# Attention scores of a head pair: two 64-row products on the halves of the array instead of one 128-row product over zero-padded keys

## The chip, the cores and the metric

The kernel runs on one core of a Trainium2 chip. The metric is device time in microseconds (us): 629.18 us, the median of 3 runs (628.95, 629.18, 633.04).

## What is computed

Two layers (DEPTH = 2) of an encoder on 256 tokens of width 1024. Each layer is an attention sublayer with 16 heads of 64 dimensions in three groups, followed by a gated feed-forward sublayer. All inputs and outputs are 32-bit floats. The attention part of the reference, cut to what matters here:

```python
qa = rms_norm(heads(qa, 4), qg[0]);  ka = rms_norm(heads(ka, 4), kg[0])
out_a = neighbourhood_attention(qa, ka, heads(va, 4), ...)   # group "a": 4 heads, bias and mask
qd, kd = partial_rotary(rms_norm(...)), partial_rotary(rms_norm(...))
out_d = dilated_window_attention(qd, kd, heads(vd, 6), ...)  # group "d": 6 heads, mask
qc, kc = axial_rotary(rms_norm(...)), axial_rotary(rms_norm(...))
out_c = gqa_block_attention(qc, kc, heads(vc, 2))            # group "c": 6 query heads on 2 key heads
...
s = einsum('bqhd,bqkhd->bhqk', q, k) * scale + bias          # the scores of one head: 256 x 256, over 64 dimensions
p = softmax(s);  o = p @ v
x = x + concat(rms_norm(out_a), rms_norm(out_d), rms_norm(out_c)) @ w_out
...
x = x + (gelu(conv(rms_norm(x) @ w_g)) * (rms_norm(x) @ w_u)) @ w_dn
```

## The kernel before

Every matrix product is made in three parts to keep the accuracy of 32-bit floats: each operand is split into a high part, rounded to the format that TensorE takes in one pass (fp32r), and the rest, a low part; `mm3` (line 544) multiplies high by high, high by low and low by high into the same PSUM tile. ScalarE writes each high part (a cast), VectorE the low part (a subtraction). This holds for the weights (`split`, line 516) as for the activations.

**Order of the work.** The program first writes all operations down (`Plan.add`, line 233) and then plans the order itself (`Plan.order`, line 278): it simulates the five engines with the costs of `cost` (line 348) and hand-over times between engines, and always takes next the operation that could begin earliest, ties going to the one written first. The result is a fixed order for each engine; an engine that comes to an operation whose inputs are missing waits there, and everything behind it waits too. PSUM tiles come from two pools of four banks: `psa` for long accumulations, `psw` for everything short, the scores among it.

**Attention of a layer.** Queries and keys of a group are normed and rotated with tokens on the partitions, then transposed on TensorE in 128-column pieces, each of which holds a pair of heads (64 + 64 rows), so a pair's 64 + 64 dimensions lie on the 128 partitions. `transposed` (line 856) moves them out of PSUM: ScalarE the high part, VectorE the low part. For the queries (`queries`, line 868) one copy takes all 128 rows. For the keys (`keys`, line 876) there are two, of 64 rows each: the tiles `kown` and `kkv` (lines 469 and 470; `const_ko` and `const_kc` in the profile) hold for each pair two blocks of 256 columns, one with the first head's keys on the upper 64 rows and zeros below, one with the second head's keys on the lower 64 rows and zeros above. The zeros are written once at the start by GpSimd (lines 471 to 473).

`scores` (line 1053) makes the scores of a pair of heads: for each of the two blocks of 128 query tokens, t, the 128-row queries of both heads are the stationary operand and the 512 columns of keys beside zeros the moving one; so one `mm3` gives the scores of both heads side by side in one PSUM tile. That is 6 products of 128 rows and 512 columns for a pair, 48 for a layer, 96 in all. A PSUM tile holds block t of both heads.

`Head.softens` (line 906) is the softmax on VectorE and ScalarE: maximum over each block t (with the bias added for groups "d" and "a"), `small_nm` from both maxima, exponentials, division. `Head.turn` (line 937) transposes the probabilities on TensorE into a `psw` tile and splits them into `act_ch` and `act_cl`; `Head.weigh` (line 953) multiplies them with the values (products of 256 columns). The loop at line 1123 writes, for each head i: the scores of a pair, the turn of head i-1, the weighing of head i-2. Behind it, as filler on TensorE, stand the products of the remaining projections (`psa_a<-...,act_hT`) and of the output projection (`psa_a<-...,act_mixT`), which the planner puts wherever TensorE would be free.

The feed-forward sublayer and the first projections of a layer use none of this.

## Time and profile before

| | |
|---|---|
| median of 3 runs | 629.18 us (628.95 to 633.04) |
| the profiled execution | 629.88 us |
| its span, first to last instruction | 627.9 us |
| TensorE clock granted | 1.0 throughout |
| TensorE products of the scores | 60 of `const_ko`, 36 of `const_kc`; the first starts at 42.7, the last at 418.0 us |
| attention of layer 0, of layer 1 | about 42 to 127 us, 345 to 432 us |

PE is TensorE's matmul stream, PEld its stream of weight loads (every matmul has one), DVE is VectorE, ACT is ScalarE, POOL is GpSimd. The ends of matmuls in the trace are modelled: matmuls follow each other faster than they "last", so how long one takes of the engine is read from the distance between two starts. A row of the timeline gives the start, the time from it to the end of the last instruction of the row, and the number of instructions merged into it. Shapes stand as rows*columns of the stationary operand, then what is written.

### The profile page before, as it was taken

What the parts mean: (1) busy time and instruction counts of PE and PEld (TensorE: products, weight loads), DVE (VectorE), ACT (ScalarE), POOL (GpSimd) and SP (SyncE); (2) the same over time, 40 slices, a digit from 0 to 9 for tenths busy, and PEclk for the clock granted to TensorE, in tenths of its full rate; (3) what the DMA queues carried; (4) which work ended last, traced back from release to release, by engine and by line L of the source; (5) the groups of instructions that cost most, each with busy time, mean ns of one, the idle gap of its engine ahead of it and who ended that gap; (6) DMA issues with size and microseconds to landing.
All of it is one profiled execution on the core that took longest, in us unless ns stands there. A gap on an engine that the chain in (4) does not pass through costs nothing.

```text
span 627.9 us, 9711 instructions
## 1 busy us (share of the span) xinstructions
PE 613.9 (98%) x3400; PEld 531.4 (85%) x3400; DVE 497.6 (79%) x1038; ACT 436.5 (70%) x1076; POOL 90.8 (14%) x139
## 2 busy tenths in 40 slices
PE   8998999989999999999999999999999999999997
PEld 6997898878888888888899989787888888888886
DVE  4899989889777777777877898988887777777775
ACT  6887998786665556656678989887766655666552
POOL 5765231340000000000013210311000000000000
PEclk9999999999999999999999999999999999999999
DMA  8794311694556655555435732134655555555511
GB/s 283 253 282 143 114 36 41 214 237 164 194 200 202 200 183 176 182 197 185 149 109 165 248 102 85 35 117 155 202 200 201 195 175 171 198 200 181 171 51 67
DMA packets 81344, 104.65 MB, mean 167 GB/s; under 512 B 9464, under 2 KB 68952, under 8 KB 81296
## 3 DMA queue, kind: packets, MB, share of 16 engines
q1 hardware_dynamic: 80720, 103.51, 51.0%
q8 instruction: 26, 0.43, 0.3%
q10 hardware_dynamic: 576, 0.53, 0.3%
q14 instruction: 22, 0.18, 0.1%
HBM read 102.54 MB, written 1.49 MB: 166 GB/s over the span
## 4 chain that ended last, share of the span: by engine, by line
PE 88%; DVE 7%; ACT 2%; issue 1%; DMA 1%; POOL 0%; ACTq 0%; DVEq 0%
PE psw_w L345 47%; PE psa_a L345 41%; DVE wp_lo L345 2%; DVE act_s2k L345 1%; DMA const_x<-in_x_dram 1%; DVE act_z L345 1%; DVE act_hT L345 1%; ACT act_s2k L345 1%; DVE small_mx L345 0%; DVE small_ss L345 0%; DVE small_nm L345 0%; DVE act_cl L345 0%; DVE const_ko L345 0%; DVE const_x L345 0%; ACT wp_hi L345 0%
## 5 line engine op out<-in xcount | busy, mean ns | idle before, releaser
L345 DVE TENSOR_TENSOR wp_lo<-wp_raw,wp_hi 128x512 fp32r<-128x512 f32 (+2 forms) x348 | 247.4, 740 | 48.8 <-ACT wp_hi L345 47.0
L345 PE MATMUL psw_w<-act_hT,wp_hi 128*128 128x512 f32 x704 | 247.3, 396 | 4.3 <-DVE act_hT L345 4.3
L345 ACT CAST wp_hi<-wp_raw 128x512 fp32r<-128x512 f32 (+2 forms) x348 | 212.9, 659 | 22.8 <-PE psw_w L345 15.5
L345 PE MATMUL psw_w<-act_hT,wp_lo 128*128 128x256 f32 x704 | 195.9, 279 | 0.0
L345 PEld LDWEIGHTS psw_w<-act_hT,wp_hi 128*128 128x128 f32 x704 | 131.8, 188 | 36.1 <-DVE act_hT L345 5.5
L345 PEld LDWEIGHTS psw_w<-act_hT,wp_lo 128*128 128x128 f32 x704 | 132.6, 188 | 1.2
L345 PE MATMUL psa_a<-wp_hi,act_hT 128*128 128x384 f32 (+2 forms) x448 | 114.8, 334 | 0.0
L345 ACT COPY act_s2k<-psw_w 128x256 f32<-128x256 f32 x88 | 32.4, 373 | 80.3 <-PE psw_w L345 80.3
L345 PEld LDWEIGHTS psa_a<-wp_hi,act_hT 128*128 128x128 f32 x448 | 79.3, 191 | 2.4
L345 PE MATMUL psa_a<-wp_lo,act_hT 128*128 128x384 f32 (+2 forms) x224 | 75.1, 335 | 0.0
L345 PE MATMUL psa_a<-wp_lo,act_ch 128*128 128x512 f32 x176 | 69.5, 395 | 0.0
L345 PE MATMUL psa_a<-wp_hi,act_ch 128*128 128x512 f32 x176 | 69.5, 395 | 0.0
L345 PE MATMUL psa_a<-wp_hi,act_cl 128*128 128x512 f32 x176 | 66.2, 395 | 0.3 <-DVE act_cl L345 0.3
L345 DVE TENSOR_TENSOR act_s2k<-psw_w,act_s2k 128x256 f32<-128x256 f32 x88 | 36.8, 422 | 30.7 <-ACT act_s2k L345 30.2
L345 PEld LDWEIGHTS psa_a<-wp_lo,act_hT 128*128 128x128 f32 x224 | 42.6, 190 | 2.6 <-DVE wp_lo L345 1.4
L345 PEld LDWEIGHTS psa_a<-wp_hi,act_cl 128*128 128x128 f32 x176 | 33.1, 188 | 8.5 <-DVE act_cl L345 0.8
L345 PEld LDWEIGHTS psa_a<-wp_hi,act_ch 128*128 128x128 f32 x176 | 33.1, 188 | 7.9 <-ACT act_ch L345 0.2
L345 PEld LDWEIGHTS psa_a<-wp_lo,act_ch 128*128 128x128 f32 x176 | 33.1, 188 | 6.9
L345 DVE SCALAR_TENSOR_TENSOR act_s2k<-act_s2k,act_cw,act_s2k 128x255 f32<-128x255 f32 x88 | 36.7, 477 | 1.4 <-ACT act_s2k L345 1.3
L345 ACT ACTIVATE act_s2k<-act_s2k,act_cw 128x256 f32<-128x256 f32 x44 | 24.1, 595 | 13.6 <-DVE act_s2k L345 13.6
L345 POOL TENSOR_TENSOR small_rstd<-small_ms,const_mh 128x6 f32<-128x6 f32 (+2 forms) x26 | 31.3, 1204 | 2.1
L345 ACT ACTIVATE act_s2k<-act_s2k 128x512 f32<-128x512 f32 x22 | 13.9, 633 | 22.5 <-DVE act_s2k L345 22.5
(112 smaller groups left out, 818.5 us busy)
## 6 DMA issues: line engine op xcount, KB each, us to landing
wp_raw<-in_w_gate_up_dram SPq DMA_DIRECT2D x44, 1024.0 KB, 5.0
wp_raw<-in_w_down_dram SPq DMA_DIRECT2D x22, 1024.0 KB, 4.7
wp_raw<-in_w_in_dram SPq DMA_DIRECT2D x14, 768.0 KB, 4.8
wp_raw<-in_w_in_dram SPq DMA_DIRECT2D x8, 1024.0 KB, 5.9
wp_raw<-in_w_out_dram SPq DMA_DIRECT2D x8, 768.0 KB, 4.6
wp_raw<-in_w_out_dram SPq DMA_DIRECT2D x4, 512.0 KB, 3.7
act_nab<-dram_scr SPq DMA_DIRECT2D x4, 448.0 KB, 8.0
out_dram<-const_x SPq DMA_DIRECT2D x4, 256.0 KB, 2.0
```

The lines of the kernel that those rows point to most:

```text
L345: getattr(o.engine.real, o.method)(*map(real, o.args), **{k: real(v) for k, v in o.kw.items()})
```

## The change

- Keys lose the zeros: one tile of 128 rows for a pair, as the queries have (`act_ko`, `act_kc` in place of `const_ko`, `const_kc`), filled by one copy on ScalarE and one subtraction on VectorE per block of tokens, both over 128 rows. `queries` and `keys` become one function, `by_pairs`. The memsets of the zeros go.
- Scores: a product takes one head's 64 rows, which are the upper (LOW) or lower (HIGH) half of the array's rows, and 256 columns of keys. For a pair there are 2 heads x 2 blocks t x 3 parts = 12 products in place of 6, alternating between the halves. A PSUM tile holds both blocks of one head.
- Burst: the planner gets `together`. The 12 products of a pair stand behind each other on TensorE with nothing between, and the first is placed only when the inputs of all 12 and both PSUM tiles are there. The planner's cost of a product with fewer than 128 rows is n / 4.8 + 15 ns.

Where this moves instructions. TensorE at the first pair of heads of layer 0 (`psw_w` are the score tiles, `act_qo` the queries; `psa_a` is filler); before, the first two products of the pair and, after twenty-two of filler, the other four:

```order
L345 MATMUL psa_a_344<-wp_hi_247,act_hT_138 128x384
L345 MATMUL psw_w_125<-const_ko_117,act_qo_452 128x512
L345 MATMUL psw_w_125<-const_ko_145,act_qo_452 128x512
L345 MATMUL psa_a_314<-wp_lo_258,act_hT_138 128x384
...
L345 MATMUL psa_a_344<-wp_hi_247,act_hT_138 128x384
L345 MATMUL psw_w_125<-const_ko_117,act_qo_459 128x512
L345 MATMUL psw_w_149<-const_ko_117,act_qo_452 128x512
L345 MATMUL psw_w_149<-const_ko_145,act_qo_452 128x512
L345 MATMUL psw_w_149<-const_ko_117,act_qo_459 128x512
L345 MATMUL psa_a_160<-wp_hi_133,act_hT_138 128x256
```

and now:

```order
L393 MATMUL psa_a_332<-wp_hi_235,act_hT_135 128x384
L393 MATMUL psw_w_123<-act_ko_574,act_qo_440 128x256
L393 MATMUL psw_w_144<-act_ko_574,act_qo_440 128x256
L393 MATMUL psw_w_123<-act_ko_584,act_qo_440 128x256
L393 MATMUL psw_w_144<-act_ko_584,act_qo_440 128x256
L393 MATMUL psw_w_123<-act_ko_574,act_qo_447 128x256
L393 MATMUL psw_w_144<-act_ko_574,act_qo_447 128x256
...
L393 MATMUL psw_w_144<-act_ko_584,act_qo_440 128x256
L393 MATMUL psw_w_123<-act_ko_574,act_qo_447 128x256
L393 MATMUL psw_w_144<-act_ko_574,act_qo_447 128x256
L393 MATMUL psa_a_154<-wp_hi_130,act_hT_135 128x256
```

The twelve products stand in one piece, where the last four stood before; their two PSUM tiles take turns.

VectorE at the same place, from the keys' low parts (`const_ko`, `act_ko`) to the maxima of the first head (`small_mx`, `small_nm`); the ISA rows add the bias and take the maximum. Before:

```order
L345 TENSOR_TENSOR const_ko_145<-psw_w_149,const_ko_117 64x3x128 x2
L345 TENSOR_TENSOR const_ko_145<-psw_w_121,const_ko_117 64x3x128 x2
L345 TENSOR_TENSOR wp_lo_258<-wp_raw_170,wp_hi_247 128x384 x4
L345 TENSOR_TENSOR wp_lo_143<-wp_raw_93,wp_hi_133 128x512 x4
L345 ISA act_s2k_202,small_mx_671<-psw_w_125,const_dil_219 128x256
L345 ISA small_mx_671 128x1
L345 TENSOR_TENSOR wp_lo_258<-wp_raw_141,wp_hi_247 128x512
L345 ISA act_s2k_202,small_mx_671<-psw_w_149,const_dil_219 128x256
L345 ISA small_mx_671 128x1
L345 TENSOR_SCALAR small_nm_692<-small_mx_671 128x2
```

and now:

```order
L393 TENSOR_TENSOR act_ko_584<-psw_w_144,act_ko_574 128x3x128
L393 TENSOR_TENSOR act_ko_584<-psw_w_119,act_ko_574 128x3x128
L393 TENSOR_TENSOR wp_lo_246<-wp_raw_164,wp_hi_235 128x384 x4
L393 TENSOR_TENSOR wp_lo_140<-wp_raw_93,wp_hi_130 128x512 x4
L393 TENSOR_TENSOR wp_lo_246<-wp_raw_138,wp_hi_235 128x512
L393 ISA act_s2k_190,small_mx_673<-psw_w_123,const_dil_207 128x256
L393 ISA small_mx_673 128x1
L393 ISA act_s2k_190,small_mx_673<-psw_w_123,const_dil_207 128x256
L393 ISA small_mx_673 128x1
L393 TENSOR_SCALAR small_nm_690<-small_mx_673 128x2
```

Four subtractions for the keys became two, and one split of weights (`wp_lo`) that stood between the two maxima now stands ahead of both; both maxima read the one tile of the first head.

TensorE at the first pair of group "c" in layer 0 (`const_ident,act_s2k` are the transposes of a head's probabilities). Before, the products of the pair stood among the transposes of the head before:

```order
L345 MATMUL psw_w_149<-const_ident_81,act_s2k_123 128x128
L345 MATMUL psw_w_89<-const_kc_173,act_qc_782 128x512
L345 MATMUL psw_w_149<-const_ident_81,act_s2k_123 128x128 x3
L345 MATMUL psw_w_89<-const_kc_190,act_qc_782 128x512
L345 MATMUL psw_w_89<-const_kc_173,act_qc_791 128x512
L345 MATMUL psw_w_121<-const_kc_173,act_qc_782 128x512
```

and now they stand ahead of them:

```order
L393 MATMUL psa_a_154<-wp_lo_246,act_hT_135 128x256
L393 MATMUL psw_w_123<-act_kc_1016,act_qc_762 128x256
L393 MATMUL psw_w_119<-act_kc_1016,act_qc_762 128x256
...
L393 MATMUL psw_w_123<-act_kc_1016,act_qc_784 128x256
L393 MATMUL psw_w_119<-act_kc_1016,act_qc_784 128x256
L393 MATMUL psw_w_89<-const_ident_81,act_s2k_150 128x128 x4
```

The transposes of that head, four in a row, now come after the whole burst.

The diff, cut to its core:

```diff
@@ class Plan
+    @contextmanager
+    def together(self):
+
+        self.burst = len(self.bursts)
+        self.bursts[self.burst] = []
+        yield
+        self.burst = None
...
@@ Plan.order
+        def at_of_burst(burst):
+            at, wanted = 0.0, {}
+            members = set(self.bursts[burst])
+            for i in self.bursts[burst]:
+                o = ops[i]
+                if any(j not in members and not gone[j] for j in o.before):
+                    return None
+                at = max(at, o.at, free[o.engine.name])
+                for t in o.tiles:
+                    if t.slot is not None:
+                        at = max(at, t.since)
+                    else:
+                        wanted.setdefault(t.pool, set()).add(t)
+            for s, tiles in wanted.items():
+                if {t.turn for t in tiles} != set(range(s.given, s.given + len(tiles))) or len(s.free) < len(tiles):
+                    return None
+                at = max(at, sorted(s.free)[len(tiles) - 1][0])
+            return at
...
                     o = ops[i]
+                    if e in opened:
+                        if o.burst != opened[e]:
                             continue
+                        at = at_of(o)
+                    elif o.burst is not None:
+                        at = at_of_burst(o.burst) if i == self.bursts[o.burst][0] else None
+                    else:
+                        at = at_of(o)
...
+            if o.burst is not None:
+                opened[e] = o.burst
+                if i == self.bursts[o.burst][-1]:
+                    del opened[e]
...
@@ cost
+        if args[1].shape[0] < P:
+            return n / 4.8 + 15, 0
         return n / (2.4 if args[1].dtype == F32R else 1.2) + 2.5, 0
...
-    LOW, HIGH = slice(0, HD), slice(HD, P)
-    kown = [const.tile([P, H_DIL // 2, 2, S], F32R, tag=f"ko{i}", name=f"ko{i}") for i in range(2)]
-    kkv = [const.tile([P, H_GKV, 2, S], F32R, tag=f"kc{i}", name=f"kc{i}") for i in range(2)]
-    for z in kown + kkv:
-        nc.gpsimd.memset(z[HIGH, :, 0].bitcast(F32), 0.0)
-        nc.gpsimd.memset(z[LOW, :, 1].bitcast(F32), 0.0)
...
-            for rows_, *both in places:
-                h, o = (z[:, :, t * P : (t + 1) * P] for z in both)
-                nc.scalar.copy(h, pv[rows_])
-                nc.vector.tensor_tensor(o, pv[rows_], h.bitcast(F32), op=ALU.subtract)
...
+            h, o = (z[:, :, t * P : (t + 1) * P] for z in both)
+            nc.scalar.copy(h, pv)
+            nc.vector.tensor_tensor(o, pv, h.bitcast(F32), op=ALU.subtract)
+
+        def by_pairs(what, group, n, zs, first=0):
 
             c = "c" if group == "c" else "o"
...
+            both = [
+                act.tile([P, 3, S], F32R, tag=f"{what}{c}{i}", name=f"{what}{i}{group}{l}", bufs=1)[:, :n]
+                for i in range(2)
+            ]
             for t in range(NT):
...
+                transposed(pairs(zs[t], first, n), both, t, f"{what}{group}{l}{t}")
             return both
...
@@ scores
-            for t in range(NT):
-                c = slice(t * P, (t + 1) * P)
-                sp = psw.tile([P, 2, S], F32, tag="w", name=f"s_{a.name}{t}")
-                mm3(sp, qh[:, c], ql[:, c], kh, kl, True, True)
-                sps.append(sp)
-            for e in range(2):
-                heads[i + e].softens([sp[:, e] for sp in sps])
+            two = heads[i : i + 2]
+            sps = [psw.tile([P, NT, S], F32, tag="w", name=f"s_{z.name}") for z in two]
+            g = two[0].group
+            with nc.together():
+                for t in range(NT):
+                    for x, y in ((0, 0), (0, 1), (1, 0)):
+                        for z, sp, rows_ in zip(two, sps, (LOW, HIGH)):
+                            nc.tensor.matmul(
+                                sp[:, t], turned[g + "q"][x][rows_, z.h // 2, t * P : (t + 1) * P],
+                                turned[g + "k"][y][rows_, z.kv if g == "c" else z.h // 2],
+                                start=(x, y) == (0, 0), stop=(x, y) == (1, 0),
+                            )
+            for z, sp in zip(two, sps):
+                z.softens([sp[:, t] for t in range(NT)])
```

More of the change, by code (lines that the diff above doesn't have):

```diff
@@ L197 @@
 class Op:
-    __slots__ = ("engine", "method", "args", "kw", "ns", "size", "tiles", "first", "before", "after", "left", "at", "rank")
+    __slots__ = ("engine", "method", "args", "kw", "ns", "size", "tiles", "first", "before", "after", "left", "at", "rank", "burst")
 class PlanEngine:
@@ L292, in order, with at_of @@
                 ready[o.engine.name].append(i)
+        def at_of(o):
+            at = max(o.at, free[o.engine.name])
+            for t in o.tiles:
+                s = t.pool
+                if t.slot is not None:
+                    at = max(at, t.since)
+                    continue
+                if t.turn != s.given or not s.free:
+                    return None
+                at = max(at, min(s.free)[0])
+            return at
[7 more added lines that the diff above has]
+                at = max(at, o.at, free[o.engine.name])
+                for t in o.tiles:
+                    if t.slot is not None:
+                        at = max(at, t.since)
+                    else:
+                        wanted.setdefault(t.pool, set()).add(t)
+            for s, tiles in wanted.items():
+                if {t.turn for t in tiles} != set(range(s.given, s.given + len(tiles))) or len(s.free) < len(tiles):
+                    return None
+                at = max(at, sorted(s.free)[len(tiles) - 1][0])
+            return at
         done = []
+        gone = [False] * len(ops)
+        opened = {}
         while len(done) < len(ops):
@@ L1001, in turn_d @@
         def turn_d(which):
-            turned["d" + which] = (queries if which == "q" else keys)(
-                "d", H_DIL // 2, [hold["d" + which, t] for t in range(NT)]
-            )
+            turned["d" + which] = by_pairs(which, "d", H_DIL // 2, [hold["d" + which, t] for t in range(NT)])
         def prep_c(which, g):
```

39 lines of the change are left out of this document (9 added, 30 removed).

## The prediction

> **What bounds the kernel now.** First the page: busy time of the engines, and the chain of work that ended last.
>
> ```profile
> PE 613.9 (98%) x3400; PEld 531.4 (85%) x3400; DVE 497.6 (79%) x1038; ACT 436.5 (70%) x1076; POOL 90.8 (14%) x139
> PE 88%; DVE 7%; ACT 2%; issue 1%; DMA 1%; POOL 0%; ACTq 0%; DVEq 0%
> ```
>
> TensorE is the bound: 88% of the chain. The change lies in the two attention stretches alone, so they come next, by window (busy time of PE, PEld, DVE, ACT, POOL, then the granted clock):
>
> ```profile
> 42.00:127.00 85.00, 82.46 (x500) 71.39 (x499) 78.14 (x212) 70.89 (x209) 27.56 (x38) 1.00 0.40 122
> 345.00:432.00 87.00, 86.09 (x531) 76.48 (x531) 76.86 (x219) 76.94 (x220) 14.83 (x21) 1.00 0.38 122
> ```
>
> PE is filled there too, at full clock, but VectorE is busy for 78.14 of 85 us and ScalarE for 76.94 of 87: a shorter TensorE has little room before they bind. What still stops TensorE in the first stretch is seen at its weight loads:
>
> ```profile
> PEld psw_w L345 <- ACT act_s2k L345: 1.1, 1, 1.1
> PEld psw_w L345 <- DVE act_z L345: 1.0, 1, 1.0
> PEld psw_w L345 <- DVE act_cl L345: 0.8, 1, 0.8
> ```
>
> Three stops of about 1 us, each behind a softmax or a rotation. So time taken off TensorE's queue in these stretches should come off the total nearly in full.
>
> **What a score product costs now.** Matmuls overlap, so I read the distance between starts, not durations. From the timeline of PE:
>
> ```profile
> 68.27 0.87 PE L345 MATMUL psw_w<-const_ko,act_qo 128*128 128x512 f32 x3
> 68.97 0.63 PE L345 MATMUL psa_a<-wp_hi,act_hT 128*128 128x512 f32 x2
> ...
> 63.76 0.28 PE L345 MATMUL psw_w<-act_cl,const_v 128*128 128x256 f32 x1
> 63.88 0.40 PE L345 MATMUL psw_w<-act_ch,const_v 128*128 128x256 f32 x2
> 64.11 0.28 PE L345 MATMUL psw_w<-act_cl,const_v 128*128 128x256 f32 x1
> 64.23 0.28 PE L345 MATMUL psw_w<-act_ch,const_v 128*128 128x256 f32 x1
> 64.36 0.63 PE L345 MATMUL psa_a<-wp_hi,act_hT 128*128 128x512 f32 x2
> ```
>
> Three score products of 512 columns take 68.97 - 68.27 = 0.70 us, a pair of heads with six 1.40 us. Five products of 256 columns take 64.36 - 63.76 = 0.60 us, 0.12 each. The groups give the number of pairs:
>
> ```profile
> L345 PE MATMUL psw_w<-const_ko,act_qo 128*128 128x512 f32 x60 | 17.6, 409 | 0.0
> L345 PE MATMUL psw_w<-const_kc,act_qc 128*128 128x512 f32 x36 | 10.6, 410 | 0.0
> ```
>
> 96 products, 16 pairs: 16 x 1.40 = 22.4 us of TensorE.
>
> **What the twelve cost.** No row shows a product on half of the rows, so I bound it. If the halves work at once, six slots of 0.12 make 0.72 us; if they take turns, twelve make 1.44. Between them stands the issue of the second product; the smallest distance of two matmul starts that I find between different operands is 0.03 us:
>
> ```profile
> 82.91 0.27 PE L345 MATMUL psw_w<-const_ident,act_s2k 128*128 128x128 f32 x1
> 82.94 0.48 PE L345 MATMUL psw_w<-const_kc,act_qc 128*128 128x512 f32 x1
> ```
>
> With it a slot of two is 0.15 and the burst 0.90 us. The weight loads double in number, 12 for 6, and may be what limits it:
>
> ```profile
> 94.83 0.52 PEld L345 LDWEIGHTS psw_w<-const_ones,act_sqm 128*128 128x128 f32 x4 [0.43 <-issue]
> 55.66 0.20 PEld L345 LDWEIGHTS psw_w<-const_ident,act_z 128*128 128x128 f32 x2 [1.03 <-DVE act_z L345]
> ...
> 95.27 0.19 PEld L345 LDWEIGHTS psa_a<-wp_hi,act_mixT_hi 128*128 128x128 f32 x1
> 53.30 0.14 PEld L345 LDWEIGHTS psw_w<-const_ident,act_s2k 128*128 128x128 f32 x1 [1.12 <-ACT act_s2k L345]
> ```
>
> Four loads with a one-column product between them stand (0.52 - 0.19) / 3 = 0.11 us apart; the two after an empty engine (0.20 - 0.14) = 0.06. (0.19 and 0.14 are the lengths of single loads, in the last two rows: of a product's weights and of a transpose's.) Twelve loads thus need 0.72 us or 1.32. I take the former, since loads for different halves don't wait for each other's products, and keep 1.32 as a bound.
>
> Against it speaks the Trainium skill, page "TensorE: Matmul & The Clock Gate", section "LDWEIGHTS (loading the stationary operand)": a load takes its columns divided by 1.2 GHz, however few the rows. That would be 107 ns for 128 columns, by my estimate 1.28 us for twelve; the 0.11 us row agrees, the 0.06 us row doesn't decide it, as a start is not an end.
>
> **Going to half the rows and back.** Only one product of the warm program works on a narrow strip of rows:
>
> ```profile
> 14.15 0.33 PE L345 MATMUL psa_a<-wp_lo,act_hT 128*128 128x384 f32 x1
> 14.32 0.34 PE L345 MATMUL psa_a<-wp_hi,act_hT 128*128 128x384 f32 x1
> 14.59 0.24 PE L345 MATMUL psw_w<-const_ident,act_s2k 32*128 32x32 f32 x1
> 14.77 0.72 PE L345 MATMUL psw_w<-const_warm 128*128 128x256 bf16 x5
> ...
> 14.59 0.13 PEld L345 LDWEIGHTS psw_w<-const_ident,act_s2k 32*128 32x128 f32 x1 [0.25 <-issue]
> 14.76 0.44 PEld L345 LDWEIGHTS <-const_warm 128*128 128x128 bf16 x5
> ```
>
> The 384-column product of 14.32 should end its turn at 14.49, as the one before took 0.17; the 32-row one starts at 14.59, 0.10 late, its load not issued ahead ("issue", 0.25). The next load comes 0.17 after it, 0.06 more than the 0.11 above. So I price both changes of a burst at 0.16 us, from one occurrence. Less than nothing is excluded, since a change of the split does no work of the kernel. The upper bound is an array that runs empty each time: a 512-column product's end behind its slot, 0.87 - 2 x 0.23 - 0.23 = 0.18 us, and a load of 0.19 that nothing hides, 0.37 a change, 0.74 a burst.
>
> Sum on TensorE: 0.90 + 0.16 = 1.06 us a burst for 1.40, 0.34 saved, 16 x 0.34 = 5.4 us.
>
> **The keys' copies.** Before, by group (the last four are the queries', of the shapes that the keys now have):
>
> ```profile
> L345 DVE TENSOR_TENSOR const_ko<-psw_w,const_ko 64x384 fp32r<-64x384 f32 x8 | 4.4, 555 | 0.6 <-ACT const_ko L345 0.4
> L345 DVE TENSOR_TENSOR const_ko<-psw_w,const_ko 64x256 fp32r<-64x256 f32 x8 | 3.4, 423 | 0.7 <-ACT const_ko L345 0.4
> L345 DVE TENSOR_TENSOR const_kc<-psw_w,const_kc 64x256 fp32r<-64x256 f32 x8 | 3.4, 422 | 0.9 <-ACT const_kc L345 0.9
> L345 ACT CAST const_ko<-psw_w 64x384 fp32r<-64x384 f32 x8 | 3.8, 475 | 0.2
> L345 ACT CAST const_ko<-psw_w 64x256 fp32r<-64x256 f32 x8 | 3.0, 369 | 0.1
> L345 ACT CAST const_kc<-psw_w 64x256 fp32r<-64x256 f32 x8 | 2.9, 362 | 0.1
> L345 DVE TENSOR_TENSOR act_qo<-psw_w,act_qo 128x384 fp32r<-128x384 f32 x4 | 2.1, 554 | 0.2
> L345 DVE TENSOR_TENSOR act_qo<-psw_w,act_qo 128x256 fp32r<-128x256 f32 x4 | 1.7, 419 | 0.0
> L345 ACT CAST act_qo<-psw_w 128x384 fp32r<-128x384 f32 x4 | 1.8, 515 | 0.4 <-PE psw_w L345 0.4
> L345 ACT CAST act_qo<-psw_w 128x256 fp32r<-128x256 f32 x4 | 1.6, 403 | 0.0
> ```
>
> A copy of 128 rows costs what one of 64 does. VectorE: 4.4 + 3.4 + 3.4 = 11.2 us become 2.1 + 1.7 + 1.7 = 5.5. ScalarE: 9.7 become 1.8 + 1.6 + 1.6 = 5.0. Both lie beside TensorE and I count them at nothing, but they are the reason why I let the 5.4 us through: VectorE gives up 5.7 of its own, so it doesn't become the bound. Without that, VectorE's 78.14 us would stand against 85 - 2.7 in the first stretch and hold part of the gain back. The memsets of the zeros are on GpSimd, which has 14% to do; nothing waits for them.
>
> **The new wait.** The burst starts only with both PSUM tiles free and all queries and keys of the pair split. Behind it on TensorE stand fillers and, as the third order shows, four transposes of the previous head, for whose split ScalarE and VectorE wait. At worst they come a burst later (1.06 us) where they stood among the score products. In return the first head's scores are whole 1.06 us after the burst's start, where they needed all six products, 1.40. I charge 0.5 us in all (bounds: 1 us gained over the stops above, 2 us lost).
>
> Total: the profiled execution's 629.88 - 5.4 + 0.5 = 625.0. That execution lies 0.70 above the median 629.18, so 624.3 against the median.
>
> **Rivals.**
>
> Full overlap: the halves start together, the burst is 0.72 + 0.16 = 0.88, 0.52 saved, 8.3 in all: 629.88 - 8.3 + 0.5 - 0.70 = 621.4. For it: products of different heads share neither rows nor PSUM banks. Against: no row shows two starts closer than 0.03. The Trainium skill, "TensorE: Matmul & The Clock Gate", section "Measured speedup vs the span model", has tiles follow each other by 4 ns, which would give this case; no run here shows it yet.
>
> No overlap worth having: the loads of both halves share one path at 0.11 us, or the products take turns. The burst is 1.32 + 0.16 = 1.48 or 1.44 + 0.16 = 1.60, 0.08 to 0.20 more than now, 1.3 to 3.2 in all: 630.5 to 632.4, say 631.4. For it: the steady 0.11 us. Against: 0.06 after an empty engine.
>
> VectorE binds: TensorE saves 5.4, but half of it turns into waits for `act_cl` and `small_nm`: 629.88 - 2.7 - 0.70 = 626.5. For it: 78.14 of 85. Against: its own 5.7.
>
> Slower: the array empties at each change of the row split and the products take turns besides. 1.44 + 0.74 = 2.18 a burst, 0.78 more, 12.5 in all: 641.7. It decides once a burst with its two changes passes 1.40 us; from 1.79 it costs over 1%. For it: the "issue" idle of 0.25 before the 32-row load. Against: that start was late by 0.10 alone.
>
> **How the numbers follow.** Forecast 0.42, full overlap 0.25, no overlap 0.20, VectorE 0.06, slower 0.07. A measurement of this kernel tells about 1%, 6.3 us, from no change. Faster by more means below 622.9: most of full overlap (0.19) and the better third of the forecast (0.13), 0.32. Slower by more is the last rival, 0.07. The rest is 0.61. The range reaches from somewhat under full overlap, 619.5, to the products taking turns, 632.5.
>
> **What would show it.** Right: 192 score products of 64 rows whose starts lie 0.07 to 0.08 us apart in a burst, some 0.9 us from the first to the last, and under 0.1 us lost at either edge; the stretch from the first scores to the last output projection some 2.5 us shorter in each layer; VectorE about 5.7 us less busy. Wrong: starts at an even 0.11 to 0.12 us (no overlap); a PEld idle of 0.3 or more at each edge (the array empties); new waits of PE for `act_cl` or `act_s2k` of several us (VectorE).

## The result and the profile after

The changed kernel takes 626.0 us (median of 8 runs, 624.93 to 627.71), the kernel before 629.5 (8 runs on the same chips, 628.95 to 633.81): ratio 0.9941, 95% interval 0.9927 to 0.9955. That is 3.5 us less, where 4.9 were forecast, and inside the range. Two of the kernels below, and the kernel before once beside them, had one execution of over 1000 us each, which is left out of what is said here. The profiled execution of the changed kernel took 626.01 us, its span 624.2.

Busy time of the engines and the chain of work that ended last, from the page of the changed kernel:

```profile
PE 608.7 (98%) x3496; PEld 525.0 (84%) x3496; DVE 490.3 (79%) x1026; ACT 430.6 (69%) x1064; POOL 83.3 (13%) x131
PE 86%; ACT 4%; DVE 4%; DMA 3%; POOL 1%; issue 1%; SPq 0%; ACTq 0%; POOLq 0%; DVEq 0%
```

TensorE is 5.2 us less busy, VectorE 7.3, ScalarE 5.9; TensorE still has 98% of the span, and 86% of the chain where it had 88%. The first attention stretch and the second, by window (columns as in the prediction):

```profile
42.00:127.00 85.00, 82.21 (x564) 70.69 (x563) 74.97 (x208) 71.22 (x213) 26.55 (x38) 1.00 0.47 139
345.00:432.00 87.00, 84.91 (x579) 72.56 (x577) 72.96 (x211) 74.22 (x214) 15.71 (x23) 1.00 0.36 119
```

In the second, TensorE is now busy for 84.91 of 87 us where it was for 86.09: it stands still for 2.1 us instead of 0.9. One burst, on TensorE's timeline:

```profile
57.99 0.49 PE L393 MATMUL psw_w<-const_ident,act_z 128*128 128x128 f32 x3
58.23 0.48 PE L393 MATMUL psa_a<-wp_hi,act_hT 128*128 128x512 f32 x1
58.65 0.97 PE L393 MATMUL psw_w<-act_ko,act_qo 64*128 64x256 f32 x12
59.55 0.50 PE L393 MATMUL psa_a<-wp_lo,act_hT 128*128 128x512 f32 x1
59.88 0.39 PE L393 MATMUL psa_a<-wp_hi,act_hT 128*128 128x512 f32 x1
60.12 0.39 PE L393 MATMUL psa_a<-wp_lo,act_hT 128*128 128x512 f32 x1
```

From the burst's start to the next product it is 59.55 - 58.65 = 0.90 us. But the product after the burst holds its slot for 59.88 - 59.55 = 0.33 where 60.12 - 59.88 = 0.24 is its pace: 0.10 at the way out. At the way in, the 384-column product ahead of the first burst of the kernel (45.90, below) is followed 0.27 later, where the pace of that shape was 0.17: another 0.10. The weight loads stand idle for a moment there ("issue", 0.25):

```profile
58.64 0.77 PEld L393 LDWEIGHTS psw_w<-act_ko,act_qo 64*128 64x128 f32 x12 [0.25 <-issue]
```

So a burst takes 0.90 + 0.10 + 0.10 = 1.10 us of TensorE for 1.40 before; all sixteen are alike, their 0.90 lying between 0.902 and 0.909. 16 x 0.30 = 4.8 us are saved.

How far the saving got is read from two starts in each layer: the first score product and the first product of the feed-forward sublayer (`act_hT,wp_hi`). Before:

```profile
42.67 0.40 PE L345 MATMUL psw_w<-const_ko,act_qo 128*128 128x512 f32 x1
130.81 0.50 PE L345 MATMUL psw_w<-act_hT,wp_hi 128*128 128x512 f32 x1 [0.65 <-DVE act_hT L345]
355.56 0.64 PE L345 MATMUL psw_w<-const_ko,act_qo 128*128 128x512 f32 x2
437.07 0.50 PE L345 MATMUL psw_w<-act_hT,wp_hi 128*128 128x512 f32 x1 [1.12 <-DVE act_hT L345]
```

After:

```profile
45.90 0.34 PE L393 MATMUL psa_a<-wp_hi,act_hT 128*128 128x384 f32 x1
46.17 0.50 PE L393 MATMUL psw_w<-act_ko,act_qo 64*128 64x256 f32 x4
126.89 0.50 PE L393 MATMUL psw_w<-act_hT,wp_hi 128*128 128x512 f32 x1 [0.18 <-DVE act_hT L393]
352.20 0.50 PE L393 MATMUL psw_w<-act_ko,act_qo 64*128 64x256 f32 x4
433.62 0.50 PE L393 MATMUL psw_w<-act_hT,wp_hi 128*128 128x512 f32 x1 [1.59 <-DVE act_hT L393]
```

Layer 0 reaches its feed-forward sublayer 130.81 - 126.89 = 3.9 us earlier. (Its stretch can't be compared as it stands: the filler that stood among the first pair's products now comes ahead of them, so the first score product starts 3.5 us later.) In layer 1 the stretch is 433.62 - 352.20 = 81.42 us, before 437.07 - 355.56 = 81.51. So the whole gain is made in layer 0; layer 1 saves eight bursts' 2.4 us on TensorE and gives them back. What TensorE waits for instead, the waits of the weight loads in layer 1 tell (the stretch from the first scores to the feed-forward sublayer; us in total, times, longest). Before, the first two of the list:

```profile
PEld psw_w L345 <- DVE act_cl L345: 1.1, 1, 1.1
PEld psw_w L345 <- issue: 0.4, 1, 0.4
```

After, the first four:

```profile
PEld psw_w L393 <- ACT act_s2k L393: 2.8, 3, 1.3
PEld psw_w L393 <- issue: 1.0, 4, 0.3
PEld psw_w L393 <- DVE const_x L393: 0.8, 2, 0.5
PEld psw_w L393 <- ACT act_ch L393: 0.7, 1, 0.7
```

Three turns now wait for their exponentials. The first of them, on ScalarE's timeline:

```profile
356.28 0.37 ACT L393 ACTIVATE const_v<-psa_a,small_rx 128x128 fp32r<-128x128 f32 x1 [1.09 <-PE psa_a L393]
356.65 1.28 ACT L393 ACT_TABLE_LOAD   x1
357.95 0.51 ACT L393 ACTIVATE act_s2k<-act_s2k,small_nm 128x256 f32<-128x256 f32 x1
```

Before, the order was the other way round:

```profile
358.65 1.28 ACT L345 ACT_TABLE_LOAD   x1
359.95 0.51 ACT L345 ACTIVATE act_s2k<-act_s2k,small_nm 128x256 f32<-128x256 f32 x1
...
360.95 0.35 ACT L345 ACTIVATE const_v<-psa_a,small_rx 128x128 fp32r<-128x128 f32 x1
```

The new plan put the scaling of the values ahead of the first exponentials, and ScalarE stands 1.09 us for it. TensorE's stops beyond its pace can be added up from the distances between starts (less 0.118 us for 256 columns, 0.173 for 384, 0.232 for 512, 0.109 for a transpose; the distances into and out of a score product and out of the product behind it are left out, since they hold the edges of a burst, which are counted above). Over the stretch of layer 1 they are 3.1 us before and 5.9 after, over that of layer 0 5.4 and 4.6. So layer 0 gains 2.4 us by its bursts, 0.8 by shorter stops and 0.7 in smaller pieces, and in layer 1 stops that are 2.7 us longer eat up the bursts' 2.4.

So the question for the experiments: does time taken off TensorE pass to the total, as the prediction said, and is the loss in layer 1 an accident of the new order, or is VectorE or ScalarE the limit there? The first theory says the former. Its rival says that the three engines are so near to balance that TensorE's saving is worth little and the 3.5 us come from the relief that the keys' copies give to VectorE and ScalarE.

### The profile page after: what moved, and what is told of

It is laid out like the page before. It is cut to its first block, busy times and chain, and to the rows that moved or that the text cites. A ratio compares the mean times of both kernels' runs of the same rounds, so it can differ in the third digit from the quotient of the medians.

```text
span 624.2 us, 9846 instructions
## 1 busy us (share of the span) xinstructions
PE 608.7 (98%) x3496; PEld 525.0 (84%) x3496; DVE 490.3 (79%) x1026; ACT 430.6 (69%) x1064; POOL 83.3 (13%) x131
## 4 chain that ended last, share of the span: by engine, by line
PE 86%; ACT 4%; DVE 4%; DMA 3%; POOL 1%; issue 1%; SPq 0%; ACTq 0%; POOLq 0%; DVEq 0%
PE psw_w L393 47%; PE psa_a L393 39%; ACT act_s2k L393 2%; DMA act_nab<-dram_scr 1%; DVE wp_lo L393 1%; DMA dram_scr<-act_nab 1%; DVE act_s2k L393 1%; POOL small_rstd L393 1%; DVE act_hT L393 1%; DMA act_s2k<-in_norm_g_dram 1%; POOL act_nab L393 0%; ACT L393 0%; ACT wp_hi L393 0%; DVE const_x L393 0%; DVE act_z L393 0%
## 5 line engine op out<-in xcount | busy, mean ns | idle before, releaser
L393 ACT ACTIVATE act_s2k<-act_s2k,small_rs 128x256 f32<-128x256 f32 x64 | 28.8, 506 | 3.3 <-DVE small_rs L393 3.3
```

The lines of the kernel that those rows point to most:

```text
L393: getattr(o.engine.real, o.method)(*map(real, o.args), **{k: real(v) for k, v in o.kw.items()})
```

## The experiments

Every kernel was timed beside the kernel before on the same chip; the ratios are to that one (629.8 to 630.0 us, where it was 629.5 beside the changed kernel). Differences in us between two kernels are between medians from different chips, and are good to about 0.5 us.

**Price of a burst, alone.** 168 products were added at the end of the changed kernel, where TensorE has nothing else; the output is not touched.

```diff
...
+    with nc.together():
+        for what, n in (
+            [(full, 256)] * 8 + [(half, 256), (top, 256)] * 6 + [(full, 256)] * 8
+            + [(half, 256)] * 6 + [(top, 256)] * 6 + [(full, 256)] * 8
+            + [(half, 256)] * 12 + [(full, 256)] * 8
...
+        ):
+            ps, r = what
+            nc.tensor.matmul(ps[:, :n], z[r, :P], z[r, :n], start=True, stop=True)
```

> The changed kernel with 166 extra products behind its last result, in a fixed order, to read the distance between starts of each pattern (128 rows: full; rows 0 to 63 and 64 to 127: low, high). Its time is longer by the tail, some 18 to 25 us, which says nothing. Theory (halves overlap when neighbours on the queue are of different halves, and only a change between full and half rows costs): low/high alternating 0.003 and 0.115 us, so 0.12 a pair; six low then six high 0.12 each, as twelve low; 24 alternating pay the same 0.4 us at the edges as 12; low, high, full, low, high, full pays the edges each time, over 0.4 us a round above the slots; at 512 columns 0.23 a pair; at 128 columns 0.06 a pair if the loads of the halves overlap too, 0.11 to 0.22 if loads share one path. Rival (the edge is a cost of the weights, not of the split): six low then six high shows edges of its own where the half changes.

The row of the tail, and below it the distances between starts in it, in ns, as read from its records (L and H are products of 64 rows on the lower-numbered and the higher-numbered half of the rows, F of 128 rows; the last distance of a list is the one to the product that follows it; the records don't name the half, so which of them is L and which H is told by the program's order and the pace):

```profile
624.63 20.91 PE L393 MATMUL psw_w<-act_ch 128*128 128x256 f32 x168 [1.49 <-ACT act_ch L393]
```

```
F x8 between half-row lists   223 118 125 113 119 120 120 210
LH x6                         4 219 3 116 3 114 3 115 3 116 3 207
LH x12                        4 220 3 114 ... 3 117 3 117 3 206
L x6, then H x6               222 119 7 110 112 6 111 8 112 120 120 206
L x12                         225 120 121 116 118 120 120 120 120 120 120 206
LHF x4                        3 313 312 4 310 313 3 310 314 3 310 223
LH x8, 128 columns            3 161 3 110 3 106 3 109 4 108 3 111 3 108 3 200
F x8, 128 columns             164 110 113 112 114 111 110 111
```

Two halves start 3 ns apart: full overlap, a pair in 0.118 us. At 128 columns a pair follows every 0.11 us, not 0.06 as was expected for loads that overlap: loads on one half still follow each other every 0.11, but those of the two halves start 3 ns apart, and two together take what one takes for 128 rows. A change of the row split costs 0.10 at the last slot before it (210 for 118, 207 for 118) and 0.10 at the first slot behind it (219, 223; only 0.05 at 128 columns, 161 and 164 for 110): 0.4 us at 256 columns for the way in and out, once for twelve products and once for twenty-four, and in each round of the list with an F between the pairs. L alone runs no faster than F. Six L and then six H take 1.25 us, 0.35 more than in turns. The fourth product to start does so 7 ns behind the third, where products of one half follow each other by 118: by that it is the first H, which begins beside the third L.

**The twelve by head, planned anew.** The same twelve products, six of one head and then six of the other.

```diff
-                for t in range(NT):
-                    for x, y in ((0, 0), (0, 1), (1, 0)):
-                        for z, sp, rows_ in zip(two, sps, (LOW, HIGH)):
+                for z, sp, rows_ in zip(two, sps, (LOW, HIGH)):
+                    for t in range(NT):
+                        for x, y in ((0, 0), (0, 1), (1, 0)):
```

> The twelve products of a burst in another order: six of the first head, then six of the second, all else as changed. Theory (only neighbours of different halves overlap): a burst takes 12 x 0.118 less one overlap plus 0.4 of edges, 1.7 to 1.8 us for 1.10, so 16 x 0.65 = 10 us more on TensorE, 634 to 637 us, slower than before the change. Rival (the halves have queues of their own and run apart): as the changed kernel, 626.

Measured: 625.4 us (624.66 to 625.57), ratio 0.9920 (0.9896 to 0.9943). Each burst takes 1.25 us, so TensorE has 16 x 0.345 = 5.5 us more to do than in the changed kernel, and yet the time is no longer. (The expected 1.7 to 1.8 us a burst was wrong, as the list above shows.) Taken by itself this spoke for the rival of the section before, by which TensorE's time is worth little. But the plan differs too: TensorE's stops, summed as above, are 3.2 and 1.7 us in the two layers where the changed kernel has 4.6 and 5.9.

**The keys copied in halves, as before.**

```diff
-            nc.scalar.copy(h, pv)
-            nc.vector.tensor_tensor(o, pv, h.bitcast(F32), op=ALU.subtract)
+            for r in (slice(0, HD), slice(HD, P)) if name[0] == "k" else (slice(0, P),):
+                nc.scalar.copy(h[r], pv[r])
+                nc.vector.tensor_tensor(o[r], pv[r], h[r].bitcast(F32), op=ALU.subtract)
```

> The keys are copied in two pieces of 64 rows each, as before the change; scores as changed. VectorE gets back some 5.7 us of work, ScalarE some 4.7. Theory (copies lie beside TensorE): 626.0 to 626.8. Rival (the gain is VectorE's and ScalarE's relief, not TensorE's): 628 or more, most of the 3.5 us lost.

Measured: 631.8 us (629.62 to 634.02), ratio 1.0026 (1.0009 to 1.0043): 5.8 us more than the changed kernel, all of the gain gone, as the rival expected. Part of it is the clock, which the windows show at half speed behind a cluster of TensorE's stops (the third number from the end of a row; DMA share and GB/s follow it):

```profile
121.00:125.00 4.00, 2.99 (x12) 2.50 (x11) 3.85 (x8) 0.75 (x2) 0.94 (x3) 0.65 0.99 326
125.00:129.00 4.00, 4.00 (x11) 3.13 (x10) 1.13 (x2) 1.00 (x2) 0.70 (x1) 0.50 1.11 326
```

Its four runs at a mean clock of 0.996 or more took 629.6 to 630.8, still about 4 us over the changed kernel.

**Exponentials first in layer 1.** The order that the rows of ScalarE above show was turned back: the values' scaling of layer 1 waits for the first head's exponentials.

```diff
...
+            if l == 1 and heads and src.shape[1] == H_GKV:
+                i, j = len(nc.ops) - 1, heads[0].exps
+                nc.ops[i].before.add(j)
+                nc.ops[i].left += 1
+                nc.ops[j].after.append(i)
...
+                self.exps = len(nc.ops) - 1
```

> One ScalarE instruction moved in layer 1: the values of group c for the first block of tokens come behind the first head's exponentials in place of ahead of them, where they waited 1.09 us for a TensorE projection. Theory (in layer 1 what TensorE saves is lost because its first turn waits for that softmax): the wait of 1.3 us before the first turn goes, 624.8 to 625.3. Rival (another wait takes its place, as at the other stops of layer 1): 625.8 to 626.2.

Measured: 626.7 us (625.7 to 627.14), ratio 0.9941 (0.9922 to 0.9961), no gain, and over both bands. The stretch of layer 1 did get shorter, from 81.42 to 432.27 - 351.56 = 80.71 us, but behind it the clock fell, which by an estimate took back more: it was at 0.5 for 3.41 us, up to 1.7 us of TensorE's work (432 to 436 us, clock 0.58). The mean clock of its six runs was 0.994 to 0.997:

```profile
432.00:436.00 4.00, 3.73 (x13) 3.20 (x14) 4.00 (x9) 3.19 (x9) 1.85 (x3) 0.58 0.04 13
```

**The kernel before with one key copy of 128 rows.** Its six products stay on 128 rows and 512 columns. The second block of keys is all zeros and the scores mix the two heads of a pair, so the attention weights are other numbers; the count and shape of the instructions is what is timed.

```diff
-        nc.gpsimd.memset(z[HIGH, :, 0].bitcast(F32), 0.0)
+        nc.gpsimd.memset(z[HIGH, :, 1].bitcast(F32), 0.0)
...
-            places = [(rows_, *(z[rows_, :, i] for z in both)) for i, rows_ in enumerate((LOW, HIGH))]
+            places = [(slice(0, P), *(z[:, :, 0] for z in both))]
```

> The kernel before with the keys' copies of the change alone: one copy of 128 rows in place of two of 64, into the first block of the zero-padded tile, the second block all zeros. The scores then mix both heads of a pair and are not the reference's; every product keeps its size and number (96 of 128 rows and 512 columns). Theory 1 (after the change VectorE and ScalarE bind, and the gain is the 5.7 and 4.7 us that they give up): 626 to 627, most of the gain. Theory 2 (the gain is TensorE's 4.8 us): 629 to 630, no gain.

Measured: 626.8 us (625.81 to 627.09), ratio 0.9950 (0.9937 to 0.9962). Together with the keys in halves, this looked like proof of the rival: relief of VectorE and ScalarE alone gives nearly the whole gain.

**Measured costs in the planner.** The traces give 0.232 us for 512 columns, where the plan reckoned 0.216, and 1.10 for a burst, where it reckoned 0.82. In the changed kernel:

```diff
-            return n / 4.8 + 15, 0
-        return n / (2.4 if args[1].dtype == F32R else 1.2) + 2.5, 0
+            return n / 4.8 + 38, 0
+        return n / (2.4 if args[1].dtype == F32R else 1.2) + (15 if args[1].dtype == F32R else 2.5), 0
```

> The changed kernel, planned with the measured costs of TensorE: n / 4.8 + 38 ns a product of 64 rows (a burst of 1.10 us), n / 2.4 + 15 one of 128. Only the order changes. Theory (the plan thinks TensorE too fast and so puts instructions that wait for it ahead of the softmax on ScalarE): 624 to 625.3. Rival (the order is not what is lost): 625.7 to 627.

Measured: 624.2 us (623.57 to 624.3), ratio 0.9908 (0.9894 to 0.9922), the fastest kernel of the study. In layer 1 the list of what the weight loads wait for has no long entry left; its first two:

```profile
PEld psw_w L393 <- issue: 0.9, 4, 0.3
PEld psw_w L393 <- ACT wp_hi L393: 0.5, 2, 0.2
```

The two starts of layer 1:

```profile
354.21 0.50 PE L393 MATMUL psw_w<-act_ko,act_qo 64*128 64x256 f32 x4
431.15 0.40 PE L393 MATMUL psw_w<-act_hT,wp_hi 128*128 128x512 f32 x1
```

The stretch of layer 1 takes 431.15 - 354.21 = 76.94 us instead of 81.42, with the same instructions and the same bursts of 0.91 us; TensorE's stops there are 1.4 us instead of 5.9, which is the whole difference. So VectorE and ScalarE can feed TensorE there: what held it up was the order. Layer 0 lost by the same plan: it reaches its feed-forward sublayer at 128.33 us, 1.4 later than in the changed kernel, and its stops did not shrink (4.7 us for 4.6). So of 4.5 us won in layer 1 the kernel keeps 1.8.

The kernel before, with the second of the two lines:

> The kernel before, planned with n / 2.4 + 15 ns a product of 128 rows; only the order changes. It is the control for the planned costs: if it gains as much as the changed kernel does with them, the costs are worth something by themselves. Theory: 628 to 629.5. Rival (orders scatter): 630 to 632.

Measured: 632.3 us (631.24 to 633.43), ratio 1.0043 (1.0027 to 1.0059). That is over both bands: better costs made a worse order there.

**No burst.** The twelve products stand free, so that the planner may put others between them.

```diff
-            with nc.together():
+            if True:
```

> The changed kernel without the burst: the planner may put other products between the twelve, and does so at about 11 of the 16 pairs, which adds a change of the row split and back at each, 0.4 us. TensorE works 4 to 5 us more. If VectorE and ScalarE bind (theory 1): 625 to 627. If TensorE binds (theory 2): 630 to 632.

Measured: 633.9 us (630.79 to 634.36), ratio 1.0056 (1.0036 to 1.0076). The sixteen bursts fell into twenty-six pieces, some of them by head. By the distances above each piece costs 0.4 us at its edges, so ten more are 4.0 us of TensorE, and with the slower pieces by head it has 6.3 more to do. The median lies over both bands; the one run at full clock took 630.8, inside the second, the others, at 0.996 to 0.997, 633.5 and more. This plan is a new one too.

At this point one thing stood out: kernels that differ in nothing but the order of the same instructions lay up to 3 us apart. Wherever the plan is made anew, its luck is as large as the effect. The last four kernels were chosen for that: two complete the table of three factors, two hold the order still.

**One key copy, measured costs.** The kernel before with one copy and the planner's costs above.

> The kernel before with one key copy of 128 rows (its scores are again products over 128 rows and 512 columns, and mix the two heads of a pair, so the attention weights are other numbers; the number and shape of the instructions is what is timed), now planned with 15 ns more for each full-rate matmul. It gave 626.8 us under the old costs; the changed kernel gave 626.0 under the old ones and 624.2 under measured ones. Theory 1 (the engines are balanced, and the plan decides how much of TensorE's shorter bursts is kept): without the shorter bursts the measured costs have less to keep, 626 to 629, at least 2 us over the changed kernel with measured costs. Theory 2 (the gain is the copies' relief of VectorE and ScalarE alone, and measured costs merely make a better order): 624 to 625.

Measured: 629.8 us (628.98 to 632.77), ratio 0.9999 (0.9987 to 1.0011). Neither band has it; it is 5.6 us over the changed kernel with the same costs, so without the shorter bursts the measured costs bring nothing. And it is 3.0 us over the same instructions with the old costs: the 626.8 of one copy alone rested on its order, too, and is no proof of the rival.

**Keys in halves, measured costs.** The changed kernel with the keys' edit and the planner's costs above.

> The changed kernel with its twelve products a burst, but with the keys copied in halves as before (5.7 us more of VectorE, 4.7 more of ScalarE), planned with the measured costs. Under the old costs it gave 631.8. Theory 1 (VectorE and ScalarE bind beside TensorE): the copies' work cannot be planned away, 628 to 631. Theory 2 (its loss was the order that the old costs chose): 624 to 626.

Measured: 627.7 us (627.11 to 629.69), ratio 0.9967 (0.9956 to 0.9979). 3.5 us over the same kernel with one copy, 4.1 under itself with the old costs: both the copies and the order counted, and neither band has it.

**The twelve by head, every order held.** The plan of the changed kernel is taken as it stands, and only within each burst the products change places. Every engine's queue is otherwise the same, instruction for instruction.

```diff
-            for i in self.order():
+            done = self.order()
+            for burst in self.bursts.values():
+                at = [k for k, i in enumerate(done) if i in set(burst)]
+                for k, i in zip(at, burst[0::2] + burst[1::2]):
+                    done[k] = i
+            for i in done:
```

> The changed kernel with its own order of every engine, instruction for instruction, except that within each burst the six products of one head come first and then the six of the other: 0.345 us more a burst, 5.5 us in sixteen. Unlike the earlier run with products by head, the plan is not made anew. Theory 1 (under the old costs TensorE's saving turns into waits of TensorE close by, so taking most of it back costs little): 626 to 628. Theory 2 (the 4.8 us that TensorE saves pass through, and the earlier run was rescued by its new plan): 630 to 631.5.

Measured: 630.9 us (628.73 to 635.27), ratio 1.0022 (1.0003 to 1.0041), 4.9 us over the changed kernel for 5.5 more on TensorE. The burst:

```profile
59.67 1.32 PE L398 MATMUL psw_w<-act_ko,act_qo 64*128 64x256 f32 x12
60.92 0.50 PE L398 MATMUL psa_a<-wp_lo,act_hT 128*128 128x512 f32 x1
```

And the two starts of each layer:

```profile
46.78 0.38 PE L398 MATMUL psw_w<-act_ko,act_qo 64*128 64x256 f32 x1
130.08 0.50 PE L398 MATMUL psw_w<-act_hT,wp_hi 128*128 128x512 f32 x1 [0.19 <-DVE act_hT L398]
356.20 0.50 PE L398 MATMUL psw_w<-act_ko,act_qo 64*128 64x256 f32 x2
440.12 0.80 PE L398 MATMUL psw_w<-act_hT,wp_hi 128*128 128x512 f32 x1 [1.59 <-DVE act_hT L398]
```

130.08 - 46.78 = 83.30 us where the changed kernel has 126.89 - 46.17 = 80.72; 440.12 - 356.20 = 83.92 where it has 81.42. The stretches grew by 2.58 and 2.50 us, and TensorE was given 8 x 0.345 = 2.76 in each: 92% passes, in layer 1 too, at a clock of 1.00 in both stretches. With the order held, TensorE's time does pass (theory 2 of this expectation), and the rival, by which it is worth little, falls. The rest of this kernel's time is partly the clock behind the attention, as in the runs above; of its twelve runs the six at a clock of 0.999 or more have a median of 630.0, 4.0 us over the changed kernel, 73% of 5.5. This is the price of TensorE's time under an order that was made for short bursts; what they would bring under the order of the kernel before isn't shown.

**The same with measured costs.** The kernel of 624.2 us, its order held in the same way.

> The changed kernel planned with measured costs (624.2 us), the order of every engine kept instruction for instruction, except that within each burst the six products of one head come first and then the six of the other. A burst gets longer by about 0.345 us as the earlier run with products by head showed, 5.5 us in sixteen. Theory 1 (with measured costs TensorE binds through the bursts): 627 to 629. Theory 2 (TensorE waits somewhere nearby in any case): 624 to 625.

Measured: 627.3 us (627.1 to 627.56), ratio 0.9954 (0.9939 to 0.9968): 3.2 of 5.5 us, 57%, in the band of theory 1 there: TensorE binds under this plan too, though less of its time passes.

All medians together (us):

| | long bursts (6 products) | short bursts (12) | short, by head |
|---|---|---|---|
| keys in halves, old costs | 629.5 (before) | 631.8 | |
| one copy, old costs | 626.8 | 626.0 (the change) | 625.4 planned anew, 630.9 order held |
| keys in halves, measured costs | 632.3 | 627.7 | |
| one copy, measured costs | 629.8 | 624.2 | 627.3 order held |

The two kernels by head with the old costs have the same instructions and the same bursts; their orders alone lie 5.5 us apart. Down and across the table the costs' edit is worth -4.1 to +3.0, the shorter bursts -5.6 to +2.3, one copy -2.5 to -5.8. Each of these has a new plan in it. Only one copy has the same sign in all four pairs, so its relief is likely to be worth something; but how much with the order held was not tried.

## Why the prediction was right

**TensorE's time passes nearly in full.** Right in kind, a little too high in size: with the order held, 4.9 of 5.5 us under the plan of the changed kernel (4.0 in the runs at full clock), 3.2 of 5.5 under the plan with measured costs.

**The burst, 1.06 us.** Measured 1.10, by two errors that nearly cancel, so that it came so near is luck. A slot of two is 0.118 us, not 0.15: the halves start 3 ns apart, not 30, as the rival of full overlap had it. The Trainium skill, "TensorE: Matmul & The Clock Gate", "Measured speedup vs the span model", has tiles follow each other by about 4 ns; the trace agrees. The row of 0.03 us that was read as the pace of issue did not show one: the product at 82.94 is followed only 0.31 later, by the next row at 83.25, so the two together took 0.34, a transpose's 0.11 and a product's 0.23. The loads don't limit the burst; the row of 0.11 us between loads holds for one half only, since pairs of 128 columns, with two loads each, also follow at 0.11. The changes of the row split were put at 0.16 us together from one product of 32 rows and 32 columns; at the burst's 256 columns they are 0.4, 0.2 at either edge where under 0.1 was to show it, and half of that stands in the burst's own first and last slot. That the loads' idle of 0.25 us at the edge comes near the 0.3 that was to tell of an empty array goes with it, but the price is 0.4 a burst, not 0.74. Saved 4.8 us for 5.4: this term was mis-sized by 0.6. Had the overlap been forecast as measured with the edges at 0.16, the full-overlap rival's 621.4 would have come out, 4.6 us too low.

**The keys' copies at nothing.** Their sizes were right:

```profile
L393 DVE TENSOR_TENSOR act_ko<-psw_w,act_ko 128x384 fp32r<-128x384 f32 x4 | 2.0, 550 | 0.0
L393 DVE TENSOR_TENSOR act_kc<-psw_w,act_kc 128x256 fp32r<-128x256 f32 x4 | 1.5, 406 | 0.0
L393 DVE TENSOR_TENSOR act_ko<-psw_w,act_ko 128x256 fp32r<-128x256 f32 x4 | 1.5, 413 | 0.0
L393 ACT CAST act_ko<-psw_w 128x384 fp32r<-128x384 f32 x4 | 1.7, 483 | 0.1
L393 ACT CAST act_ko<-psw_w 128x256 fp32r<-128x256 f32 x4 | 1.4, 372 | 0.0
L393 ACT CAST act_kc<-psw_w 128x256 fp32r<-128x256 f32 x4 | 1.3, 356 | 0.0
```

VectorE 5.0 us for 5.5 forecast, ScalarE 4.4 for 5.0. That their relief adds nothing to the time is shown only together with the new order, by one comparison: the kernel by head with the order held has bursts of 1.25 + 0.2 = 1.45 us, 0.05 more than the kernel before (0.8 us in sixteen), and all the rest of the change. It takes 630.9 us, 1.4 more than the 629.5 of before (0.9 more than the kernel before had beside it, 629.9); less those 0.8, relief and new order together come to +0.1 to +0.6. A relief that gains and an order that loses as much would look the same. With plans made anew one copy brought 2.5 to 5.8 us, so "nothing" is not a property of the copies. Whether the relief was needed to let TensorE's saving through, as the prediction reasoned, is not settled: with keys in halves the short bursts brought 632.3 - 627.7 = 4.6 us under the measured costs, but lost 2.3 under the old ones, and each of the four has a plan of its own.

**The new wait, +0.5.** No stop at a burst's start stands out; the price came elsewhere. The list of operations had changed, the planner made another order, and in layer 1 that order has 2.7 us more of stops (5.9 for 3.1), of which three turns that wait for exponentials are the largest entry. By the 4.9 of 5.5 the bursts' 4.8 us are worth 4.3; the change brought 3.5; so the rest of it costs 0.8 where 0.5 was charged (by the 4.0 of the runs at full clock the bursts are worth 3.5, and the rest costs nothing). The size was near, the place was wrong: "some 2.5 us shorter in each layer" failed, it was 3.9 and 0.

So of the 1.4 us between forecast and result, 0.6 is the burst's price, and 0.8 the share that did not pass and the new order together; 0.5 and 0.3 by the medians, 1.3 and -0.5 by the runs at full clock. The rival in which VectorE binds came nearest in number, 626.5, and its sign (new waits of TensorE, here for `act_s2k`) is in the trace; but its mechanism, VectorE at its limit, is not what stops TensorE: with measured costs the same instructions feed it through layer 1 (in layer 0, where the stops stayed, this isn't shown). No overlap and the empty array fell with the first burst's starts.

Why the clock falls to a half behind the attention in some kernels and some runs of one kernel is open. The change with the tail, whose instructions up to there are the same as the change's, was at 0.50 from 434.98 us for 3.41 us, and the change itself stayed at 1.00 in its profiled execution. The kernel by head, with the same order and the same wait of 1.59 us, fell to 0.57 in the four us behind it:

```profile
436.00:440.00 4.00, 2.31 (x13) 1.38 (x11) 3.74 (x7) 3.73 (x11) 0.16 (x1) 1.00 0.70 269
440.00:444.00 4.00, 3.88 (x13) 3.35 (x14) 4.00 (x9) 3.04 (x8) 1.85 (x3) 0.57 0.10 29
```

## What to carry to other kernels

Pack 64-row products in pairs on the two halves, in turns and in long unbroken pieces: the second product of a pair is nearly free, each piece costs 0.4 us, so that six pairs save 0.3 us and two would lose (0.64 us for 0.46, by these figures). Where a planner sets the order, any edit draws a new order that may be worth as much as the edit (here two orders of the same instructions lay 5.5 us apart): to price an edit, hold the order and change only the one thing. A comparison of two plans doesn't show the price. Measured costs in the planner are worth a try and no more: they brought 1.8 and 4.1 us with short bursts and lost 2.8 and 3.0 with long ones.

## What the runs showed of the hardware

- The halves run apart from each other, not only at once: with six products of L ahead of six of H in the program, H's first began 0.35 us behind L's first, 7 ns after L's third and ahead of L's fourth (the records don't name the half; this is read from the distances, and the bursts of the kernels by head show nearly the same ones).
- Loads for the two halves overlap: they start 3 ns apart, and pairs of 128 columns, two loads each, follow every 0.11 us, the pace of a single load for 128 rows.
- A change of the row split costs 0.10 us in the last slot before it and 0.10 in the first slot behind it, for 12 products and for 24; with 512 columns too (the last product of such a pair 315 and the next full one 335 ns, for 232), while at 128 columns the first slot behind it costs 0.05 (161 and 164 ns for 110).
- The granted clock fell to 0.5 after several stops of TensorE of at most 1.8 us each, with work between them (436 to 440 us above: busy for 2.31 of 4). Others followed one longer stop, of 2.1 us in the same kernel and of 3.1 in that with the keys in halves and the measured costs; one of 2.0 us in the changed kernel with measured costs had no fall behind it. Such falls lasted 3.41 us in five of the kernels here, and once 6.83, in the one with the keys in halves and the old costs.
